# Hybrid trunk layer on one core: the second product of each seven-product unit moved up, branch weights fetched a tile ahead, the last row's norm at high priority

## The chip, the core and the metric

The kernel runs on one core of a Trainium2 chip, in one launch. The metric is the device time of that launch in microseconds (us), as the median of several runs. The kernel before takes 1981.67 us (3 runs, 1977.3 to 1984.02). The engines are called by the names of the profile: PE multiplies matrices (PEld is its loading of weights), DVE, ACT and POOL work on vectors, SP only issues transfers; ACT issues transfers too. An engine works through its own list of instructions in order, and waits between engines are made with semaphores.

## The reference, cut to what matters

One layer of a decoder trunk with 1024 channels, 1024 tokens (16 meta tokens ahead of them) and a feed-forward width of 4096. Four mixers work side by side on the normalised input, each result is projected, weighted with its own gate and summed; an output projection, a residual and a squared-ReLU feed-forward part follow.

```python
h = rmsnorm(x, norm1_g)
proj = jnp.einsum('bld,dc->blc', h, w_in)
(..., gate_logits) = jnp.split(proj, split_at, axis=-1)
branches = (hgrn2_mixer(...), multiscale_pool(...), stick_breaking_attention(...), short_conv_mixer(...))
gates = jax.nn.sigmoid(gate_logits.astype(F32)).reshape(B_, L, N_BRANCH, D_MODEL)
mixed = jnp.zeros((B_, L, D_MODEL), F32)
for n in range(N_BRANCH):
    mixed = mixed + gates[:, :, n] * jnp.einsum('blw,wd->bld', branches[n], w_branch[n]).astype(F32)
x = x + jnp.einsum('bld,de->ble', mixed.astype(x.dtype), w_o)
h2 = rmsnorm(x, norm2_g)
act = jnp.square(jax.nn.relu(jnp.einsum('bld,df->blf', h2, w_up)))
return x + jnp.einsum('blf,fd->bld', act, w_down)
```

The output is the norm of the last x, without the leading tokens.

## The kernel before

Every large matrix is held as a rounded part and a remainder (`hi` and `lo`, made by a cast on ACT, L77, and a subtraction on DVE, L78), so that a product of two blocks is three matmuls: hi by hi, hi by lo, lo by hi. The stages come one after the other: mixers, gates, branches (each mixer's result times its `w_branch`, times its gate, summed in `mixed`), output projection, up projection, down projection.

**The seven-product unit.** In the gates and in the up projection the product of a weight block and the activations is done by a scheme of Strassen's kind, in units of a 256 by 1024 result, `strassen_run`. A unit has seven products of 12 matmuls each (4 blocks along the inner axis, 3 matmuls for each), all matmuls 128x512, in three accumulators of PSUM: `al_` (tag mm, 3 buffers), `be` (tag z, 2 buffers), `ga` (tag tr, 2 buffers). Products 1, 6, 7 and 4 go into `al_`, one upon the other, 5 and 3 into `be`, 2 into `ga`. ACT copies what stands in an accumulator between two products (`keep_copy`, L720): c1 after product 1, c5 after product 5, c2 after product 6. The next product may go into the accumulator only when the copy is made: product 6 waits for c1, product 7 for c2, product 3 for c5. The four quarters of the result are taken out by `put`: (0,0) from `ga` and c1, (1,1) from `al_` and c5, (0,1) from `be` and c2, (1,0) from `al_` alone.

In the code the products stand as 1, 5, 6, 2, 7, 3, 4. There are 20 units in the gates stage and 14 in the up stage. `ahead()` in the middle of a unit writes the load of the next unit's weights (`strassen_load`): two transfers on SP's queue (`raw` a, L685, and `raw` b, L687), then additions and casts that make the seven left operands: `hi` and `lo` for products 1 and 2, `sh` and `sl` for 5 and 6 and, in a second pair, for 3 and 7, `eh` and `el` for 4. POOL does the additions (L692 to L697), and a buffer of `raw` is free for the next load when they are done.

**The list of each engine.** The order in which an engine works through its instructions is fixed when the kernel is built: a scheduler goes through the instructions of all engines by a priority that follows the order of the code, and takes on each engine what its own estimate finds ready first. So a product may stand elsewhere in PE's list than in the code, and two products may be interleaved.

**After a unit.** In the gates stage ACT applies the sigmoid and sends each result of 128x1024 to DRAM (L852). In the up stage ACT applies relu (L990, L993) and the square (L998), DVE makes three sums (L1004 to L1007), and ACT issues seven transfers of 256 KB to `sum_dram` (L1012), the left operands of the down projection's own seven products.

**The branches.** For each of four branches, `load_branch` reads the branch's four blocks of 128x1024 (`raw` or `sf` to `b_hi` and `b_lo`), and for each of eight tiles of 128 channels `load_branch_w` reads a weight tile (`cc`, 3 buffers, to `eh` and `el`, 2 buffers each); 24 matmuls in two chunks, and DVE multiplies with the gate (`go`, read back from `gate_dram`, L877) into `mixed` (L884).

**The end.** The down projection's last unit, `Unit.end`, normalises the last rows in `final`: a square sum on ACT, a few small operations, two multiplications and the transfers of the output.

Of the kernel before, what the change touches and what calls it, by code (L numbers as in the profile page):

```python
# [20 lines left out]
KD = D // P  # L21
# [26 lines left out]
def hybrid_trunk_kernel(ctx: ExitStack, tc: tile.TileContext, x_tok, metas, vecs, gains, w_in, w_br, w_pool,  # L48
# [21 lines left out]
    def new(pl, shape, dt, tag, bufs=None):  # L70
        return pl.tile(shape, dt, tag=tag, name=nm(tag), **({} if bufs is None else {"bufs": bufs}))
# [136 lines left out]
    with ExitStack() as st:  # L208
# [222 lines left out]
        for i in range(NS + 2):  # L431
            parts, z, r = [], iter(()), i % (2 * NB)
# [272 lines left out]
    def strassen_run(pl, lhs, hi, lo, th, tl, put, ahead, tail=None):  # L705
        def blk(k0, c0):
            return hi[:, k0:k0 + 4, c0:c0 + 512], lo[:, k0:k0 + 4, c0:c0 + 512]

        rhs = {1: blk(0, 0), 2: blk(4, 0), 3: blk(4, 512), 4: (th[3], tl[3]), 5: (th[0], tl[0]), 6: (th[1], tl[1]),
               7: (th[2], tl[2])}  # L710

        def prod(ps, i, fresh):
            for k in range(4):
                for n, (x, y) in enumerate(((0, 0), (0, 1), (1, 0))):
                    nc.tensor.matmul(ps, lhs[i][x][:, k, :], rhs[i][y][:, k, :], start=fresh and k == 0 and n == 0,  # L715
                                     stop=k == 3 and n == 2, skip_group_check=not fresh)

        def keep_copy(ps):
            c = new(pl, [P, 512], F32, "cc", 3)
            nc.scalar.copy(c, ps)  # L720
            return c

        al_, be, ga = bank("mm"), bank("z"), bank("tr")
        prod(al_, 1, True)
        c1 = keep_copy(al_)
        prod(be, 5, True)
        c5 = keep_copy(be)
        nxt = ahead()
        prod(al_, 6, False)
        c2 = keep_copy(al_)  # L730
        prod(ga, 2, True)
        put(0, 0, ga, c1)
        prod(al_, 7, False)
        put(1, 1, al_, c5)
        if tail is None:
            prod(be, 3, False)
            put(0, 1, be, c2)
            prod(al_, 4, False)
            put(1, 0, al_, None)
        else:  # L740
            c7 = keep_copy(al_)
            de = bank("av")
            prod(de, 4, True)
            put(1, 0, de, c7)
            tail()
            prod(be, 3, False)
            put(0, 1, be, c2)
        return nxt
# [33 lines left out]
    with ExitStack() as st:  # L782
# [3 lines left out]
        parts = {}  # L786
# [83 lines left out]
        for i, n in enumerate(order):  # L870
            if i:
                load_branch(i)
            bh, bl = parts[i]
            for dt in range(KD):
                wb = load_branch_w(i, dt) if dt else parts[i, 0]
                sg = new(p2, [P, T], F32, "go", 3)
                nc.sync.dma_start(sg, gate_dram[n, dt])  # L877
                for c0, w in QCH:
                    cs = slice(c0, c0 + w)
                    pb = bank("mm")  # L880
                    for k in range(4):
                        mm3(pb, (wb[0][:, k, :], wb[1][:, k, :]), (bh[k][:, cs], bl[k][:, cs]), k == 0, k == 3)
                    if i == 0:
                        nc.vector.tensor_mul(mixed[:, dt, cs], pb, sg[:, cs])  # L884
                    else:
                        nc.vector.tensor_mul(sg[:, cs], pb, sg[:, cs])
                        nc.vector.tensor_add(mixed[:, dt, cs], mixed[:, dt, cs], sg[:, cs])
# [39 lines left out]
    with ExitStack() as st:  # L927
# [151 lines left out]
        class Unit:  # L1079
# [37 lines left out]
            def end(self, prev):  # L1117
# [17 lines left out]
                final(self.m + 4, 1)  # L1135
                self.prod(self.be, 3)
                nc.vector.tensor_add(self.acc(0, 1), self.be, self.acc(0, 1))
                final(self.m, 1)

        NU = (NF - FS) // 2  # L1140
        for spot, ps in held:
# [102 lines left out]
```

## Time and profile before

| | before |
|---|---|
| median of 3 runs | 1981.67 us |
| the profiled execution, its own time | 1980.0 us |
| its span in the profile | 1978.2 us |
| PE busy, share of the span | 1931.9 us, 98% |
| mean granted clock of PE, share of full speed | 0.996 |
| gates stage, 20 units (677.0 to 1056.7 us) | 379.7 us, of which PE busy 377.3 |
| first 18.3 us of the branches (1056.7 to 1075.0) | PE busy 16.0 us |
| up stage, 14 units (1374.7 to 1641.1) | 266.4 us, of which PE busy 266.4 |

The span runs from the first to the last instruction of the profiled execution; its own time is 1.8 us more. A row of the timeline gives the start of an instruction, its duration, engine and line, what it writes and reads, and in brackets how long its engine stood idle ahead of it and what released it. A group of matmuls on PE overlaps: each lasts some 0.39 us and the next starts 0.227 us later when nothing is waited for, so that a product of 12 takes 2.72 us and a unit of 84 takes 19.04 us.

### The profile page before, as it was taken

Reading aid. Unit: us, or ns where it says so; the run is one execution under the profiler, and the core shown is the slowest. Engines: PE = TensorE matmul, PEld = TensorE weight load, DVE = VectorE, ACT = ScalarE, POOL = GpSimd, SP = SyncE. Lnnn points to the kernel's source line nnn. Section 1 sums busy time; section 2 is a strip of 40 time slices with the busy share of each in tenths; the row PEclk is TensorE's granted clock in tenths of the full one; section 3 lists DMA queues with packets and bytes.
Section 4 is the critical chain, followed back from the end, with each engine's and each line's share of the span. In section 5 each row is a group of like instructions: output and inputs, shape, how many; then the busy total and the mean of one; then the engine's idle time right before and its main releaser. Section 6 shows DMA issues by size and latency. Waiting matters only on the chain.

```text
span 1978.2 us, 25779 instructions
## 1 busy us (share of the span) xinstructions
PE 1931.9 (98%) x9974; PEld 1647.4 (83%) x9974; DVE 1291.9 (65%) x1783; ACT 844.0 (43%) x1452; POOL 329.1 (17%) x280
## 2 busy tenths in 40 slices
PE   8999999999999999999999999999999999999998
PEld 7889899988899888888887888888888887777876
DVE  6677877666768844344334667479555546888887
ACT  6556654233324433333342112255544544343445
POOL 1000001111000033333320000000323212322322
PEclk9999999999999999999999999999999999999999
DMA  3000101110102233333326554242454557343433
GB/s 140 33 33 22 43 33 49 54 43 26 40 33 91 85 149 117 139 123 112 128 104 231 186 187 169 77 143 93 136 170 138 155 165 258 127 145 135 152 138 137
DMA packets 112076, 224.61 MB, mean 114 GB/s; under 512 B 8129, under 2 KB 58817, under 8 KB 111954
## 3 DMA queue, kind: packets, MB, share of 16 engines
q1 hardware_dynamic: 56706, 175.22, 25.9%
q10 hardware_dynamic: 55248, 47.75, 7.2%
q8 instruction: 78, 1.28, 0.3%
q14 instruction: 44, 0.36, 0.1%
HBM read 157.40 MB, written 65.54 MB: 113 GB/s over the span
## 4 chain that ended last, share of the span: by engine, by line
PE 76%; DVE 9%; issue 9%; DMA 3%; ACT 2%; POOL 1%; POOLq 0%; DVEq 0%; ACTq 0%; SPq 0%
PE mm L715 18%; PE mm L104 9%; PE mm L103 9%; PE mm L102 9%; PE z L715 9%; PE tr L715 5%; PE mm L1092 3%; PE z L1092 2%; PE av L362 1%; PE z L582 1%; DVE wb L78 1%; PE tr L1092 1%; DVE keep L339 1%; DVE wa L78 1%; DMA raw<-in_w_dn_dram 1%
## 5 line engine op out<-in xcount | busy, mean ns | idle before, releaser
L102 PE MATMUL mm<-h_hi,hi 128*128 128x384 f32 (+4 forms) x880 | 303.0, 345 | 1.4 <-DVE a L198 1.0
L103 PE MATMUL mm<-h_lo,hi 128*128 128x384 f32 (+4 forms) x880 | 295.2, 336 | 1.1 <-DVE h_lo L78 1.1
L104 PE MATMUL mm<-h_hi,lo 128*128 128x384 f32 (+4 forms) x880 | 295.8, 336 | 0.0
L103 PEld LDWEIGHTS mm<-h_lo,hi 128*128 128x128 f32 x880 | 166.6, 189 | 7.9 <-DVE h_lo L78 1.9
L104 PEld LDWEIGHTS mm<-h_hi,lo 128*128 128x128 f32 x880 | 166.0, 189 | 8.0
L102 PEld LDWEIGHTS mm<-h_hi,hi 128*128 128x128 f32 x880 | 166.0, 189 | 7.9 <-DVE a L198 1.4
L78 DVE TENSOR_TENSOR sl<-sf,sh 128x1024 fp32r<-128x1024 f32 x68 | 83.8, 1232 | 128.8 <-ACT sh L77 128.8
L692 POOL TENSOR_TENSOR sf<-raw 128x512 f32<-128x512 f32 x30 | 40.3, 1342 | 764.1 <-DMA raw<-in_w_up_dram 459.3
L78 DVE TENSOR_TENSOR lo<-raw,hi 128x1024 fp32r<-128x1024 f32 x76 | 95.7, 1259 | 45.2 <-ACT hi L77 44.8
L77 ACT CAST hi<-raw 128x1024 fp32r<-128x1024 f32 x76 | 79.9, 1052 | 77.0 <-PE mm L103 40.7
L715 PE MATMUL mm<-th,sh 128*128 128x512 f32 x272 | 106.2, 390 | 0.0
L77 ACT CAST sh<-sf 128x1024 fp32r<-128x1024 f32 x68 | 71.4, 1052 | 81.3 <-PE z L715 41.7
L715 PE MATMUL mm<-tl,sh 128*128 128x512 f32 x272 | 105.8, 389 | 0.0
L715 PE MATMUL mm<-th,sl 128*128 128x512 f32 x272 | 105.8, 389 | 0.0
L339 DVE TENSOR_TENSOR_SCAN keep<-keep 128x1040 f32<-128x1040 f32 (+3 forms) x64 | 88.9, 1390 | 25.7 <-ACT keep L332 18.9
L102 PE MATMUL mm<-b_hi,eh 128*128 128x512 f32 x256 | 99.6, 390 | 1.8 <-DVE mixed L884 1.8
L103 PE MATMUL mm<-b_lo,eh 128*128 128x512 f32 x256 | 100.1, 391 | 0.1
L104 PE MATMUL mm<-b_hi,el 128*128 128x512 f32 x256 | 99.6, 390 | 0.5 <-DVE el L78 0.5
L78 DVE TENSOR_TENSOR el<-raw,eh 128x512 fp32r<-128x512 f32 x34 | 36.2, 1064 | 64.5 <-ACT eh L77 61.3
L334 POOL TENSOR_SCALAR_AFFINE_SELECT keep<-keep 128x128 f32<-128x128 f32 x64 | 22.3, 348 | 300.2 <-ACT keep L332 260.2
L77 ACT CAST at_h<-tr 128x384 fp32r<-128x384 f32 (+2 forms) x112 | 54.5, 495 | 36.6 <-PE tr L349 34.9
L77 ACT CAST s_hi<-s_raw 128x1280 fp32r<-128x1280 f32 x28 | 35.4, 1266 | 80.9 <-DMA s_raw<-sum_dram 45.8
(439 smaller groups left out, 5019.2 us busy)
## 6 DMA issues: line engine op xcount, KB each, us to landing
raw<-in_w_in_dram SPq DMA_DIRECT2D x76, 512.0 KB, 3.7
s_raw<-sum_dram SPq DMA_DIRECT2D x28, 896.0 KB, 4.8
gate_dram<-go ACTq DMA_DIRECT2D x32, 512.0 KB, 2.6
go<-gate_dram SPq DMA_DIRECT2D x32, 512.0 KB, 3.7
raw<-in_w_up_dram SPq DMA_DIRECT2D x32, 512.0 KB, 3.8
raw<-in_w_dn_dram SPq DMA_DIRECT2D x29, 512.0 KB, 4.4
sum_dram<-go ACTq DMA_DIRECT2D x52, 256.0 KB, 4.7
sum_dram<-sums ACTq DMA_DIRECT2D x39, 256.0 KB, 4.8
```

Of the source, the lines that this page charges most:

```text
L77: nc.scalar.copy(hi, src)
L78: (eng or nc.vector).tensor_sub(lo, src, hi.bitcast(F32))
L102: nc.tensor.matmul(ps, lh, rh, start=first, stop=False)
L103: nc.tensor.matmul(ps, lh, rl, start=False, stop=False)
L104: nc.tensor.matmul(ps, ll, rh, start=False, stop=last)
L334: nc.gpsimd.affine_select(out=t[:, :P], in_=t[:, :P], compare_op=ALU.is_gt, fill=1.0, base=0, pattern=[[1, P]], channel_multiplier=-1)
L339: nc.vector.tensor_tensor_scan(t, t, t, 1.0, op0=ALU.mult, op1=ALU.min)
L362: nc.tensor.matmul(av[:, :w], pair.vv[e][:, b, :], a[:, b, :w], start=i == 0 and a is at[0], stop=i == len(order) - 1 and a is at[1])
L582: nc.tensor.matmul(ps[:, c * 64:(c + 1) * 64], xc, low, start=True, stop=True)
L692: eng.tensor_add(s12[:, 0], a21, a22)
L715: nc.tensor.matmul(ps, lhs[i][x][:, k, :], rhs[i][y][:, k, :], start=fresh and k == 0 and n == 0, stop=k == 3 and n == 2, skip_group_check ...
L1092: nc.tensor.matmul(ps, x, y[:, rs], start=fresh and k == 0 and n == 0, stop=k == 1 and n == 2, skip_group_check=not fresh)
```

## The change

It has three parts. In `strassen_run` product 2 and the `put` of (0,0) are written directly behind product 1, so that the order in the code is 1, 2, 5, 6, 7, 3, 4. In the branches the load of a tile's weights is written one tile earlier, ahead of the tile's gate load and matmuls. The last `final` of the kernel stands in a block of high priority, which lets the scheduler take its instructions before others that are ready.

```diff
@@ strassen_run
         al_, be, ga = bank("mm"), bank("z"), bank("tr")
         prod(al_, 1, True)
         c1 = keep_copy(al_)
+        prod(ga, 2, True)
+        put(0, 0, ga, c1)
         prod(be, 5, True)
         c5 = keep_copy(be)
         nxt = ahead()
         prod(al_, 6, False)
         c2 = keep_copy(al_)
-        prod(ga, 2, True)
-        put(0, 0, ga, c1)
         prod(al_, 7, False)
         put(1, 1, al_, c5)
@@ branches
             for dt in range(KD):
-                wb = load_branch_w(i, dt) if dt else parts[i, 0]
+                wb = parts.pop((i, dt))
+                if dt + 1 < KD:
+                    parts[i, dt + 1] = load_branch_w(i, dt + 1)
                 sg = new(p2, [P, T], F32, "go", 3)
@@ Unit.end
-                final(self.m, 1)
+                with tc.high_priority():
+                    final(self.m, 1)
```

Lines of the changed kernel stand two or three further down than those of before from L878 on: L884 becomes L886, L990 L992, L998 L1000, L1012 L1014.

**PE in a gates unit.** PE's list around product 7 of a unit in the middle of the gates stage. The names are accumulator, left operand, right operand: `h_hi_93` is the activations (products 1, 2 and 3), `th` and `tl` their sums (the others), `sh` and `sl` the weights' sums. Before, where product 2 ends and product 7 begins:

```order
L715 MATMUL tr_8692<-h_hi_93,hi_8595 128x512
L715 MATMUL tr_8692<-h_lo_94,hi_8595 128x512
L715 MATMUL tr_8692<-h_hi_93,lo_8596 128x512
L715 MATMUL mm_8690<-th_887_5926,sh_8609 128x512 [waits Activation_49]
L715 MATMUL mm_8690<-tl_890_5929,sh_8609 128x512
L715 MATMUL mm_8690<-th_887_5926,sl_8610 128x512 [waits DVE_49]
```

And of the change, from the end of product 6 to the beginning of product 7 of the same unit:

```order
L715 MATMUL mm_8690<-tl_889_5928,sh_8617 128x512
L715 MATMUL mm_8690<-th_886_5925,sl_8618 128x512
L715 MATMUL z_8691<-h_hi_93,sh_8623 128x512 [waits Activation_49]
L715 MATMUL z_8691<-h_lo_94,sh_8623 128x512
L715 MATMUL z_8691<-h_hi_93,sl_8624 128x512 [waits DVE_49]
L715 MATMUL z_8691<-h_hi_93,sh_8623 128x512
L715 MATMUL z_8691<-h_lo_94,sh_8623 128x512
L715 MATMUL z_8691<-h_hi_93,sl_8624 128x512
L715 MATMUL z_8691<-h_hi_93,sh_8623 128x512
L715 MATMUL mm_8690<-th_887_5926,sh_8623 128x512 [waits Activation_49]
L715 MATMUL mm_8690<-tl_890_5929,sh_8623 128x512
```

All 12 matmuls of product 2 stood between 6 and 7 before; after, seven matmuls of product 3 stand there (its other five come between 7 and 4), in every unit of the gates and of the up stage but the last of either. Only the first unit of the gates is in PE's list as it was: there the list of before has 1, 2, 5, 6, seven of 3, 7, five of 3, 4 as well. In the up stage the first matmuls of the next unit's product 1 (one in the second unit, one more in each that follows) come to stand between products 5 and 6 of a unit.

**ACT in an up unit.** ACT's list from the result quarter (1,0) of one unit to the copies of the next, early in the up stage; `cc<-mm` is c1 or c2, `cc<-z` is c5, the DMA rows are the transfers to `sum_dram`, of which `go_12088`, the last, is the seventh; a DMAHW in brackets is a wait for an earlier transfer with the same semaphore. Before:

```order
L998 ACTIVATE go_12088<-go_12088 128x1024 [waits Activation_49]
L720 COPY cc_12246<-mm_12231 128x512 [waits PE_49]
L1012 DMA sum_dram<-go_12088 128x4x128 [waits Activation_49]
L1012 DMA sum_dram<-go_12087 128x4x128 [waits DMAHW1_49,DVE_49]
L1012 DMA sum_dram<-sums_12217 128x4x128 [waits DMAHW2_49,DVE_49]
L1012 DMA sum_dram<-sums_12217 128x4x128 [waits DVE_49]
L1012 DMA sum_dram<-go_12088 128x4x128 [waits DMAHW4_49]
L720 COPY cc_12260<-z_12232 128x512 [waits PE_49]
L77 CAST eh_12284<-raw_12264 128x512
L77 CAST sh_12274<-sf_12270 128x1024 [waits PE_49,Pool_49]
L720 COPY cc_12300<-mm_12231 128x512 [waits PE_49]
```

Of the change:

```order
L77 CAST eh_12298<-raw_12278 128x512 [waits DMAHW6_49,PE_49]
L992 ACTIVATE go_12088<-mm_12089 128x512 [waits PE_49]
L1014 DMA sum_dram<-go_12087 128x4x128 [waits Activation_49]
L1000 ACTIVATE go_12088<-go_12088 128x1024 [waits Activation_49]
L1014 DMA sum_dram<-sums_12217 128x4x128 [waits DVE_49]
L1014 DMA sum_dram<-go_12088 128x4x128 [waits Activation_49]
L1014 DMA sum_dram<-go_12087 128x4x128 [waits DMAHW2_49,DVE_49]
L1014 DMA sum_dram<-sums_12217 128x4x128 [waits DMAHW3_49,DVE_49]
L1014 DMA sum_dram<-sums_12217 128x4x128 [waits DVE_49]
L1014 DMA sum_dram<-go_12088 128x4x128 [waits DMAHW5_49]
L720 COPY cc_12246<-mm_12231 128x512 [waits PE_49]
L720 COPY cc_12274<-z_12232 128x512 [waits PE_49]
```

The copy c1 (`cc_12246`) stood ahead of the last five transfers, and stands behind all seven. The transfer that the seventh waits for (same semaphore) is another one too: before, `raw` b of the next weights; after, `raw` a, whose cast `hi` follows in ACT's list behind c1. The seventh transfer of each of the first twelve units is like that, and c1 stands behind it in units 2 to 13. Between c5 and c2 ACT now also has the cast `hi` and a relu; the relu of (1,1) stands ahead of the second `sh` cast, where before it was the cast of `hi` that stood ahead of both.

**DVE at the start of the branches.** DVE's list in the first tiles of the first branch; `mixed` rows multiply with the gate, `el` is the remainder of a weight tile, `b_lo` that of a branch block, those with 977x and 978x belonging to the second branch. Before:

```order
L884 TENSOR_TENSOR mixed_9487<-mm_9490,go_9488 128x512 [waits DMAHW7_49,PE_49]
L884 TENSOR_TENSOR mixed_9487<-mm_9504,go_9488 128x512 [waits PE_49]
L78 TENSOR_TENSOR el_9521<-cc_9518,eh_9520 128x512 [waits DMAHW1_49,DVE_49,Activation_49]
L78 TENSOR_TENSOR el_9557<-cc_9554,eh_9556 128x512 [waits DMAHW3_49,DVE_49,Activation_49]
L78 TENSOR_TENSOR b_lo_9773<-sf_9770,b_hi_9772 128x1024 [waits DMAHW0_49,Activation_49]
L78 TENSOR_TENSOR b_lo_9785<-sf_9782,b_hi_9784 128x1024 [waits DMAHW1_49,Activation_49]
L884 TENSOR_TENSOR mixed_9487<-mm_9526,go_9524 128x512 [waits DMAHW2_49,PE_49]
```

Of the change:

```order
L78 TENSOR_TENSOR el_9491<-cc_9488,eh_9490 128x512 [waits DMAHW1_49,DVE_49,Activation_49]
L886 TENSOR_TENSOR mixed_9487<-mm_9496,go_9494 128x512 [waits DMAHW7_49,PE_49]
L886 TENSOR_TENSOR mixed_9487<-mm_9510,go_9494 128x512 [waits PE_49]
L78 TENSOR_TENSOR el_9527<-cc_9524,eh_9526 128x512 [waits DMAHW5_49,DVE_49,Activation_49]
L78 TENSOR_TENSOR b_lo_9773<-sf_9770,b_hi_9772 128x1024 [waits DMAHW6_49,Activation_49]
L886 TENSOR_TENSOR mixed_9487<-mm_9532,go_9530 128x512 [waits DMAHW1_49,PE_49]
```

The second tile's `el` stood behind the first tile's two multiplications and stands ahead of them; of the second branch's two `b_lo` ahead of the second tile's multiplications only one is left. On SP's queue the second branch's second block is now read after three more gate tiles. Ahead of these rows, at the very start, the first tile's `el` has moved behind one `b_lo`.

At the end of the kernel no engine's list differs between the two kernels: the block of high priority moves nothing.

## Rows read from the trace of the kernel before

**Rows 1.** The page, part 1: busy us (share of span), instructions.

```profile
PE 1931.9 (98%) x9974; PEld 1647.4 (83%) x9974; DVE 1291.9 (65%) x1783; ACT 844.0 (43%) x1452; POOL 329.1 (17%) x280
```

**Rows 2.** Windows: gates and up stage; busy us per engine, clock, DMA share, GB/s.

```profile
677.00:1056.70 379.70, 377.31 (x1658) 311.71 (x1657) 161.47 (x163) 149.80 (x214) 112.18 (x72) 1.00 0.34 125
...
1374.70:1641.10 266.40, 266.40 (x1177) 220.63 (x1177) 141.34 (x160) 134.79 (x185) 68.26 (x48) 1.00 0.52 151
```

**Rows 3.** Timeline of PE, first gates unit; then the window behind it, columns as above.

```profile
679.80 0.80 PE L715 MATMUL z<-th,sh 128*128 128x512 f32 x1 [2.39 <-ACT sh L77]
...
679.80:683.30 3.50, 3.50 (x9) 2.68 (x10) 3.43 (x4) 3.47 (x4) 0.00 (x0) 0.57 0.59 222
```

**Rows 4.** Timeline, first unit of the gates, seven of product 3, then product 7.

```profile
686.79 0.39 PE L715 MATMUL z<-h_hi,sh 128*128 128x512 f32 x1
...
686.81 1.05 ACT L77 CAST sh<-sf 128x1024 fp32r<-128x1024 f32 x1 [1.72 <-PE mm L715]
...
687.76 0.57 ACT L720 COPY cc<-mm 128x512 f32<-128x512 f32 x1
...
688.15 0.39 PE L715 MATMUL z<-h_hi,sh 128*128 128x512 f32 x1
688.39 0.19 PEld L715 LDWEIGHTS mm<-th,sh 128*128 128x128 f32 x1 [0.28 <-ACT cc L720]
...
688.73 0.39 PE L715 MATMUL mm<-tl,sh 128*128 128x512 f32 x1
```

**Rows 5.** Timeline of ACT, end of one up unit and start of the next.

```profile
1448.21 1.05 ACT L77 CAST sh<-sf 128x1024 fp32r<-128x1024 f32 x1 [1.19 <-PE z L715]
...
1453.85 0.57 ACT L720 COPY cc<-mm 128x512 f32<-128x512 f32 x1
1453.97 1.09 ACTq L1012 DMA_DIRECT2D sum_dram<-go  x2
1455.43 1.54 ACTq L1012 DMA_DIRECT2D sum_dram<-sums  x2
1457.01 1.32 ACTq L1012 DMA_DIRECT2D sum_dram<-go  x1
1458.37 0.59 ACT L720 COPY cc<-z 128x512 f32<-128x512 f32 x1 [3.95 <-issue]
```

**Rows 6.** Timeline of PE, same stretch: first matmul of products 1 and 6.

```profile
1450.90 0.39 PE L715 MATMUL mm<-h_hi,hi 128*128 128x512 f32 x1
...
1456.34 0.39 PE L715 MATMUL mm<-th,sh 128*128 128x512 f32 x1
```

**Rows 7.** Timeline of POOL, then of SP's queue, same stretch.

```profile
1451.85 1.74 POOL L697 TENSOR_TENSOR sf<-raw,sf 128x512 f32<-128x512 f32 x1
...
1453.62 0.33 SPq L685 DMA_DIRECT2D raw<-in_w_up_dram  x1
1460.23 0.33 SPq L687 DMA_DIRECT2D raw<-in_w_up_dram  x1
```

**Rows 8.** L685 in the up stage (12 transfers): issue to landing.

```profile
DMA to landing us min/median/max: 3.5/4.3/5.8
```

**Rows 9.** Transfers in the up stage by line: KB each, median us to landing.

```profile
sum_dram<-sums ACTq DMA_DIRECT2D x39, 256.0 KB, 4.8
```

**Rows 10.** Waits of PE, 1056.7 to 1075 us: us in total, times, longest.

```profile
PE mm L102 <- DVE mixed L884: 1.8, 1, 1.8
PE mm L104 <- DVE el L78: 0.5, 1, 0.5
```

**Rows 11.** Timeline of DVE, start of the branches.

```profile
1062.29 1.37 DVE L884 TENSOR_TENSOR mixed<-mm,go 128x512 f32<-128x512 f32 x2 [1.10 <-PE mm L104]
1063.58 1.28 DVE L78 TENSOR_TENSOR el<-cc,eh 128x512 fp32r<-128x512 f32 x2
1070.46 2.51 DVE L78 TENSOR_TENSOR b_lo<-sf,b_hi 128x1024 fp32r<-128x1024 f32 x2 [5.59 <-ACT b_hi L77]
```

**Rows 12.** Timeline of SP's queue, start of the branches.

```profile
1064.41 5.00 SPq L877 DMA_DIRECT2D go<-gate_dram  x3
```

## The prediction

> **What bounds the kernel now.** I read the page first: PE is busy for 98% of the span, DVE, at 65%, is next [rows 1]. A sum over the whole kernel doesn't say what a stage loses, so I went to the windows of the two stages with seven-product units. In the up stage PE's busy time equals the window: 266.4 of 266.4 us; in the gates 377.3 of 379.7 [rows 2]. All of the gates' idle time is one wait at the first unit's product 5, 2.39 us for the cast `sh`; in the 3.5 us behind it the granted clock is 0.57 (mostly the lower level, 1.2 of 2.4 GHz) and 9 matmuls run, 1.46 us more than 9 x 0.227 [rows 3]. So the reader is to see that units 2 to 20 of the gates and all of the up stage lose nothing now. An order of products can't gain there; it can only lose. What can be gained lies at the first unit and at the start of the branches, where PE waits 1.8 us for `mixed` and 0.5 us for `el` [rows 10].
>
> **Product 2 in the gates.** No matmul is added, removed or resized. The first unit stays as it is in PE's list, so its wait of 2.39 us stays: gain 0. For the other units the trace of before has a sample, because the first unit ran in the new order. Between products 6 and 7 product 2 gave ACT 12 matmuls, 2.72 us, for the copy c2; now seven of product 3 give 7 x 0.227 = 1.59 us. When product 6 ends, at 686.79, ACT begins the next `sh` cast (its buffer is read by 6), 1.05 us, and only then copies c2, 0.57 us, from 687.76. The weight load of product 7 waits 0.28 us for it, to 688.39, and the matmul behind starts 0.34 us after the first, not 0.227 [rows 4]. From the last matmul of product 3 (688.15) to the second of 7 (688.73) there are 0.58 us where 2 x 0.227 = 0.45 would do: 0.13 us lost, with the next row's rounding 0.15. The order on ACT is the same in each unit (`sh`, then c2), so I take 0.15 x 18 units = +2.7 us. Its lower end is 0, if c2 just makes it; its upper end 0.3 for a unit, +5.4, if the semaphores fall less luckily.
>
> **Product 2 in the up stage.** The same short cover costs 0.15 x 12 = +1.8 us (0 to 3.6).
>
> The larger matter is c1. Let T be the end of product 4, 1450.90 in the shown unit [rows 6]. Before, ACT copied c1 at 1453.85 for 0.57 us, to T + 3.5, and product 6 began at 1456.34, T + 5.44: 1.9 us to spare [rows 5, 6]. In the new list c1 stands behind all seven transfers to `sum_dram`. Product 6 is now due after products 1, 2 and 5 and one matmul of the unit after, 37 x 0.227 = 8.4 us after T, or 36 where one is fewer: I use 8.28. Before, the last issue began at 1457.01 and lasted 1.32 us, to T + 7.43 [rows 5]. With c1 behind it, 7.43 + 0.05 + 0.57 = T + 8.05: 0.2 us to spare, if that were all.
>
> It isn't, because the seventh transfer now waits for the landing of `raw` a. Before, that load was issued at 1453.62, T + 2.72, as POOL ended its second addition [rows 7]. That chain begins with the second `sh` cast at 1448.21, T - 2.69 [rows 5]; the relu of (1,1), about 0.6 us, now stands ahead of it. Product 7 now ends five matmuls before product 3 does, T - 2.72 - 1.13 = T - 3.85; an addition on DVE and the relu follow, for pieces as large as the copy c1, 0.57 us [rows 5], so with hand-overs some 0.7 each (my estimate), and the cast begins at some T - 2.3. POOL and the load are 0.4 us later: T + 3.15. The load lands 4.3 us after issue, 3.5 to 5.8 [rows 8]. It travels among the sums, which take 4.8 [rows 9], and `raw` b, which went out 6.6 us behind it (1460.23) [rows 7], now goes right behind. I take the sums' figure, nearer to a crowd: T + 7.9. Then an issue (0.4 to 1.3, say 0.45) and c1: 7.9 + 0.45 + 0.57 + 0.05 = T + 8.97. That is 0.7 us late; the restart adds 0.11 as in [rows 4]: 0.8 us for each of units 2 to 13, 12 x 0.8 = +9.6 us. Ends: with a landing after 3.5 us c1 comes at T + 7.7, cost 0; with 5.8 us it is late by 1.6, with the restart 1.7, +20 us.
>
> The row of the long issue also meets a rule. Five issues from 1453.97 on took 1.09 + 1.54 + 1.32 = 3.95 us of ACT's time, and the c5 copy behind them waited as long [rows 5]. The Trainium skill's page "DMA: Bandwidth & Descriptors", section "Issuing engines are not separate DMA queues", says that initiating a transfer takes the sequencer a time that "is usually small relative to the DMA itself". By that, seven issues ahead of c1 would cost next to nothing and this term would be 0, the sum +3.8; here the trace disagrees, with 3.95 us of issuing beside 4.8 us of landing. I go by the trace.
>
> **The ends of the stages.** In the last up unit c2 stands behind a cast that waits for a row's load; from the 4.3 us of [rows 8] against cover of a product or two I estimate +1.0 (0 to 3). In the first units of both stages another order of casts gives 0 to 0.6: +0.3.
>
> **Branch weights.** `el` of the second tile stood behind two multiplications (from 1062.29), and ran at 1063.58 [rows 11]; now it stands ahead of them, its data there as `cc` is loaded early: the wait of 0.5 us and its restart go, -0.6. The wait of 1.8 us came from DVE's list: two `b_lo` of the second branch, released by ACT at 1070.46 after 5.59 us of idling and running until 1072.97, stood ahead of the second tile's `mixed`, whose accumulator PE needed [rows 11]. Now one `b_lo` stands there, so some 1.2 us go at least, and both perhaps; but the gate tile must be in too, and its load's issue, 1064.41, waits for its write as before [rows 12]. Against this the first tile's `el` comes behind one `b_lo`, up to 1.2 us later. I take -1.4 for the pair: together -2.0 us, from -2.8 (all of [rows 10] with two restarts) to +0.5 (the first tile's delay and nothing gained).
>
> **The last norm.** No engine's list differs there, so nothing is hidden or shortened: 0.
>
> **Sum.** +2.7 + 1.8 + 9.6 + 1.0 + 0.3 - 2.0 = +13.4 us. The profiled execution took 1980.0 us, so 1993.4; that one is 1.7 below the median of 1981.67, to which I add the same: **1995 us**.
>
> **Rivals.**
> *c1 is in time.* The lateness is the difference of two figures near 8 us: with a landing at the fast end, or sums sent less densely, it vanishes, and what is left is 13.4 - 9.6 = +3.8, some 1985.5 us. For it: the 3.5 us of the minimum, and the 0.2 us to spare without the wait. Against it: the median of 4.3 still gives 3.15 + 4.3 + 0.45 + 0.62 = T + 8.5, late by 0.25 and a restart, +4 us over the 12 units. Chance 0.22.
>
> *c1 is later still.* Each late copy pushes the transfers of its unit together with both loads. Landing at 5.8 us, or an issue of 1.3 us in place of 0.45, makes 1.7 us a unit: 12 x 1.7 = 20, in place of 9.6: 2005 us. Waits as long as that of [rows 3], 2.39 us, would bring the lower clock as well, 1.46 us each time; three such would make 2009, and six 2014. Chance 0.15.
>
> *Faster.* The moved product pays only if the first unit's wait goes. If the casts of that unit came earlier with the changed lists, 2.39 + 1.46 us, in all about 4 us, would be saved, with -2.8 at the branches, and no unit lost anything at products 6 and 7: 1975 us. It decides if c2 is copied within 1.59 us of product 6's end and c1 before T + 8.3. Against it: [rows 4] show c2 late in the same order, and the first unit's list is unchanged. Chance 0.07.
>
> *The change does nothing* holds for the block of high priority, with near certainty, and is in the sum; for the whole it would need all terms at their lower ends, and lies within the first rival.
>
> **How the numbers follow.** The forecast, c1 late by 0.25 to 1.3 us, has 0.56 and covers 1987 to 2001. From no change 0.3%, some 6 us, can be told. Faster by more: 0.07, the third rival. Within it (1975.7 to 1987.6): the first rival, 0.22, and a little of the forecast's lower edge, 0.02: 0.24. Slower: 0.69. The range reaches from 1982 to 2008: out of it are the third rival (0.07), the first rival's lower part (0.04) and the tail of the second (0.06).
>
> **What would show it.** In the changed kernel's up stage the waits of PE should list "mm L715 <- ACT cc L720" some 24 times, half with 0.5 to 1 us at product 6 and half with 0.2 to 0.3 at product 7; the timeline of ACT should have c1 right behind an issue, 8.5 us or more after product 4's end, and a seventh issue that begins at the landing of L685's load. The up window should grow by 12 us, the gates' by 3. At the branches both rows of [rows 10] should be gone or shorter. I'm wrong if c1 begins before T + 7.7 in most units, if the first unit of the gates no longer waits, or if PE waits for something else in the middle of the gates, where the cast `hi` now stands ahead of c5 and is covered only as long as its load lands early.

## The result, and the profile after

| | before | after |
|---|---|---|
| median | 1981.08 us (4 runs) | 1995.72 us (4 runs, 1994.97 to 1999.94) |
| ratio to before, 95% interval | | 1.0075 [1.0062, 1.0089] |
| span of the profiled execution | 1978.2 us | 1993.4 us, 15.2 longer |
| PE busy, share of the span | 98% | 97% |
| mean granted clock | 0.996 | 0.997 |

The change makes the kernel slower by 0.75%. The windows of the changed kernel, cut at the same matmuls as those of [rows 2], with the stretches between them added, say where (columns as there):

```profile
677.13:1059.49 382.36, 379.69 (x1658) 309.16 (x1656) 160.02 (x162) 146.67 (x213) 97.69 (x72) 1.00 0.34 124
1059.49:1376.83 317.34, 314.91 (x1410) 258.08 (x1409) 216.35 (x322) 101.61 (x153) 0.00 (x0) 1.00 0.46 160
1376.83:1653.79 276.96, 272.88 (x1177) 218.69 (x1177) 151.35 (x160) 132.26 (x185) 67.83 (x48) 1.00 0.51 144
1653.79:1993.40 339.61, 317.70 (x1370) 256.32 (x1368) 279.47 (x378) 142.60 (x210) 95.30 (x64) 0.99 0.45 155
```

Beside before's, of which the two that [rows 2] lack stand here:

```profile
1056.70:1374.70 318.00, 315.08 (x1410) 258.08 (x1409) 216.45 (x322) 102.25 (x153) 0.00 (x0) 1.00 0.46 160
...
1641.10:1978.20 337.10, 317.36 (x1370) 256.45 (x1368) 279.36 (x377) 142.23 (x210) 94.68 (x64) 0.99 0.45 155
```

So the gates grew by 2.7 us, the up stage by 10.6, everything between them shrank by 0.7, and the down stage, whose instructions are the same, grew by 2.5. In the up stage PE's busy time is no longer that of the window, and PE's waits name one cause. This is the list of waits of PE in the up window, then that of its weight loads, which carry the wait for a free accumulator (us in total, times, longest):

```profile
PE mm L715 <- ACT cc L720: 3.7, 11, 0.5
```

```profile
PEld mm L715 <- ACT cc L720: 12.5, 24, 0.9
PEld z L715 <- ACT cc L720: 0.6, 1, 0.6
```

24 waits for a copy, twelve at product 6 and twelve at product 7. One of the former, in ACT's timeline of one unit:

```profile
1461.69 1.35 ACTq L1014 DMA_DIRECT2D sum_dram<-sums  x2
1464.80 0.37 ACTq L1014 DMA_DIRECT2D sum_dram<-go  x1
1465.21 0.58 ACT L720 COPY cc<-mm 128x512 f32<-128x512 f32 x1 [6.03 <-DMA raw<-in_w_up_dram]
1465.69 0.59 ACT L720 COPY cc<-z 128x512 f32<-128x512 f32 x1
1466.17 1.06 ACT L77 CAST hi<-raw 128x1024 fp32r<-128x1024 f32 x1
```

The sixth issue ends at 1463.05, the seventh begins only at 1464.80, and c1 stands behind it with 6.03 us of idling put down to the landing of `raw`. That load's row on SP's queue, the time to landing of the eleven such loads in units 2 to 12 (the first unit's took 3.5 us), and the matmuls of PE that waited:

```profile
1459.82 0.33 SPq L685 DMA_DIRECT2D raw<-in_w_up_dram  x1
```

```profile
DMA to landing us min/median/max: 4.7/4.8/5.0
```

```profile
1465.00 0.39 PE L715 MATMUL mm<-h_hi,hi 128*128 128x512 f32 x1
1465.85 0.50 PE L715 MATMUL mm<-th,sh 128*128 128x512 f32 x1 [0.46 <-ACT cc L720]
1466.19 0.40 PE L715 MATMUL mm<-tl,sh 128*128 128x512 f32 x1
```

1459.82 + 4.8 = 1464.6, then the hand-over and the seventh issue. In unit 13 no such load is left, and the seventh issue stands behind a load of the down stage. Product 6 begins 0.85 us after the matmul ahead of it, where 0.227 would do: 0.62 us lost, and 0.11 more at the next.

### The profile page after: what moved, and what is told of

The parts are those of the page before. It is cut to its first block, busy times and chain, and to the rows that moved or that the text cites. A ratio compares the mean times of both kernels' runs of the same rounds, so it can differ in the third digit from the quotient of the medians.

```text
span 1993.4 us, 25820 instructions
## 1 busy us (share of the span) xinstructions
PE 1940.8 (97%) x9974; PEld 1642.8 (82%) x9974; DVE 1300.6 (65%) x1783; ACT 837.9 (42%) x1452; POOL 314.9 (16%) x280
## 4 chain that ended last, share of the span: by engine, by line
PE 67%; DVE 12%; issue 8%; DMA 6%; ACT 4%; POOL 2%; SPq 0%; ACTq 0%; DVEq 0%; POOLq 0%
PE mm L715 15%; PE mm L104 9%; PE mm L103 9%; PE mm L102 9%; PE z L715 7%; PE mm L1094 3%; PE tr L715 3%; DMA raw<-in_w_up_dram 2%; PE av L362 2%; PE z L1094 2%; PE z L582 1%; DMA s_raw<-sum_dram 1%; DVE wb L78 1%; PE tr L1094 1%; DVE wa L78 1%
## 5 line engine op out<-in xcount | busy, mean ns | idle before, releaser
L715 PE MATMUL mm<-th,sh 128*128 128x512 f32 x272 | 111.1, 408 | 3.9 <-ACT cc L720 3.7
L720 ACT COPY cc<-mm 128x512 f32<-128x512 f32 x70 | 40.7, 582 | 112.9 <-DMA raw<-in_w_up_dram 53.2
L715 PEld LDWEIGHTS mm<-th,sh 128*128 128x128 f32 x272 | 51.0, 187 | 27.8 <-ACT cc L720 18.2
```

## The experiments

Each kernel was timed in five rounds beside the kernel before; ratios are to before, with their 95% interval. Stage times are windows of the profiled execution, cut at the same matmuls.

**c1 ahead of the transfers.** The changed kernel, with

```diff
-        def keep_copy(ps):
+        def keep_copy(ps, first=False):
             c = new(pl, [P, 512], F32, "cc", 3)
-            nc.scalar.copy(c, ps)
+            if first:
+                with tc.high_priority():
+                    nc.scalar.copy(c, ps)
+            else:
+                nc.scalar.copy(c, ps)
             return c
...
-        c1 = keep_copy(al_)
+        c1 = keep_copy(al_, True)
```

> The changed kernel with one difference: the copy c1 of each unit is written at high priority, so ACT's list has it ahead of the last six transfers to sum_dram in place of behind all seven; the first matmuls of the next unit are no longer interleaved, and c2 still stands behind the sh cast. My theory (product 6 is late by 0.6 us in twelve up units because c1 stands behind a transfer that waits for the landing of raw a): product 6's loss goes, product 7's 0.15 us stays, so the up stage is 2 to 3.5 us longer than before in place of 10.6, and the time is some 7 us under that of the change: 1988 to 1989.5 us. Rival (the new order of products itself, or the transfers' load on memory, costs the 10 us): no difference, 1994 to 1998.

Measured: 1.0154 [1.0140, 1.0168], 2013.9 us: 18 us slower than the change by the medians, 16 by the ratios, against both expectations. Product 6 loses nothing any more, as the theory has it, but the up stage takes 291.4 us, 25.0 over before. Its weight loads' waits there:

```profile
PEld z L715 <- ACT cc L724: 15.7, 12, 2.4
PEld mm L715 <- ACT cc L724: 10.6, 13, 0.9
```

The wait has moved to product 3 (z), and to product 7 behind it. ACT's timeline shows c5, the last row, behind the same seventh transfer and a relu:

```profile
1464.73 0.59 ACT L722 COPY cc<-mm 128x512 f32<-128x512 f32 x1 [0.58 <-PE mm L715]
1464.73 1.57 ACTq L1018 DMA_DIRECT2D sum_dram<-go  x2
1466.67 2.33 ACTq L1018 DMA_DIRECT2D sum_dram<-sums  x3
1469.03 2.51 ACTq L1018 DMA_DIRECT2D sum_dram<-go  x1
1472.41 0.63 ACT L999 ACTIVATE go<-go 128x512 f32<-128x512 f32 x1 [7.10 <-DVE go L998]
1472.95 0.57 ACT L724 COPY cc<-z 128x512 f32<-128x512 f32 x1
```

In the changed kernel c5 stood right behind c1, ahead of cast and relu; with c1 gone ahead, the scheduler put the relu between the issues and c5. So c1's place was a cause, but freeing it alone uncovers the next copy in the same list. Two things end late ahead of c5 here, the seventh issue (1471.54) and the relu, whose addition on DVE waits for earlier transfers out of its buffer.

**Six issues on ACT.** The changed kernel, with the third transfer of each up unit but the last issued by POOL:

```diff
-                eng.dma_start(dst[:, i], t.rearrange("p (m t) -> p m t", m=4))
+                (nc.gpsimd if i == 2 and f + 2 < NF else eng).dma_start(dst[:, i], t.rearrange("p (m t) -> p m t", m=4))
```

> The changed kernel with one of the seven transfers of each up unit but the last issued by POOL in place of ACT. c1 still stands behind all transfers that ACT issues (six), but the last of them shares no semaphore with raw a any more and doesn't wait for its landing. My theory (the wait for the landing makes c1 late): product 6's loss goes entirely, since the sixth issue then ends some 6 us after the unit's start: up stage 2 to 3.5 us longer than before, time 1988 to 1989.5 us. Rival (standing behind so many issues makes c1 late, the landing only coincides): one issue of 0.37 us fewer leaves some 0.2 of 0.6 us in each of twelve units and the restart, up stage 6 to 7 us longer than before, 1991.5 to 1993.

Measured: 1.0043 [1.0029, 1.0056], 1991.6 us; up stage 272.8 us, 6.4 over before. ACT's timeline in one unit:

```profile
1461.28 1.40 ACTq L1014 DMA_DIRECT2D sum_dram<-sums  x2
1462.72 0.59 ACT L720 COPY cc<-mm 128x512 f32<-128x512 f32 x1 [3.96 <-PE tr L715]
1464.44 1.05 ACT L77 CAST hi<-raw 128x1024 fp32r<-128x1024 f32 x1 [1.13 <-DMA raw<-in_w_up_dram]
1466.30 0.63 ACT L995 ACTIVATE go<-go 128x512 f32<-128x512 f32 x1 [0.81 <-DVE go L994]
1466.84 0.57 ACT L720 COPY cc<-z 128x512 f32<-128x512 f32 x1
```

c1 follows the sixth issue at once, and no product 6 of the stage is late: with one issue fewer and no shared semaphore the whole 0.63 us of a unit goes, not the 0.4 that one issue takes. That is the theory's side on product 6. The edit takes away an issue and the shared semaphore together; the sizes tell them apart. The stage time agrees with the rival's 6 to 7, but from another place: the wait for the landing now stands at the cast `hi`, 1.13 us, ahead of c5, and product 3 loses 5.5 us over the stage, up to 1.2 in one unit. The landing of `raw` a matters wherever in ACT's list something waits for it.

**All issues on SP.** The changed kernel, with `eng = nc.sync` for all seven transfers of every unit.

> The changed kernel with all seven transfers of every up unit issued by SP in place of ACT, so that no copy stands behind an issue; c1 is early, and in ACT's list a relu of quarter (0,0) stands ahead of c5, its addition waiting for earlier transfers out of the same buffer to land. The kernel with c1 first lost 25 us in the up stage, at product 3 and then product 7. Theory now (the wait for the buffers, brought forward with quarter (0,0), makes c5 late): product 3 still loses, up stage 5 to 15 us over before, 1989 to 2000 us. Rival (the issues on ACT ahead of c5 cost it): up stage 2 to 3.5 us over before, only product 7's share, 1987 to 1989.

Measured: 1.0024 [1.0013, 1.0035], 1986.6 us. The up window:

```profile
1377.62:1646.49 268.87, 268.87 (x1177) 219.47 (x1176) 152.52 (x160) 133.87 (x184) 67.80 (x48) 1.00 0.50 150
```

2.5 us over before, all of it in front of product 7: the rival's figure. No product 6 and no product 3 is late. Of the 10.6 us of the change 8.1 are therefore the price of issuing these transfers, with their waits, from the engine that also makes the copies. The expectation, that a relu's wait for buffers would still cost product 3, falls: it is there (0.58 us in front of the relu), but c5 comes in time. SP also sends the sums earlier, so how much of the first experiment's wait at c5 was the issue and how much the buffers stays open.

**c2 made by DVE.** The changed kernel, with `nc.vector.tensor_copy` for c2.

> The changed kernel with the copy c2 made by DVE in place of ACT, so that it stands behind no sh cast; as a consequence the scheduler also puts c1 ahead of five of the seven transfers and all of product 3 or four of its matmuls ahead of product 7. My theory (product 7 loses 0.15 us in 31 units because c2 stands behind a cast that begins when product 6 ends): both losses of the units go, gates stage as long as before (379.7 us, the wait of 2.4 us at its first unit included), up stage within 1 us of before, time 1980 to 1983 us. Rival (the short cover costs product 7 its 0.15 us whoever copies, since DVE's own list holds c2 up as well): gates 2 to 4 us longer than before, time 1984 to 1988.

Measured: 1.0109 [1.0095, 1.0123], 2004.6 us; gates 382.7 us, as in the change, up stage 287.0. A miss: the copy then stands in DVE's list behind a remainder that waits for ACT's cast, and product 7 waits for it, as DVE's timeline and PE's row show:

```profile
1471.45 1.23 DVE L78 TENSOR_TENSOR lo<-raw,hi 128x1024 fp32r<-128x1024 f32 x1 [1.52 <-ACT hi L77]
1472.59 0.68 DVE L720 COPY cc<-mm 128x512 f32<-128x512 f32 x1
```

```profile
1473.33 0.50 PE L715 MATMUL mm<-th,sh 128*128 128x512 f32 x1 [1.40 <-DVE cc L720]
```

It doesn't settle what product 7 waited for in the change; the next two do.

**The gates alone.** The kernel before, with product 2 moved up only in the units of the gates (a flag of `strassen_run`).

> The kernel before with product 2 moved up in the 20 units of the gates alone; up stage, branches and end as before. My theory: product 7 loses 0.15 us in 18 units since c2 stands behind a cast, gates stage 2.6 to 2.9 us longer, up stage 266.4 us as before: 1984 to 1986 us, some 0.13% over before. Rival (the stages aren't separate: what the up stage lost in the changed kernel begins with the state that the gates leave): up stage longer by 3 us or more, 1988 and above.

Measured: 1.0020 [1.0011, 1.0029], 1985.5 us; the windows of gates and up stage:

```profile
677.31:1059.69 382.38, 379.70 (x1658) 309.14 (x1656) 159.85 (x162) 146.82 (x213) 97.78 (x72) 1.00 0.34 124
...
1376.40:1642.80 266.40, 266.40 (x1177) 220.63 (x1177) 141.65 (x160) 135.01 (x185) 68.65 (x48) 1.00 0.52 151
```

The gates take what they take in the change, the up stage what it took before. The stages are separate.

**The gates alone, c2 ahead of the cast.** As the last, with

```diff
-                for n, (x, y) in enumerate(((0, 0), (0, 1), (1, 0))):
+                for n, (x, y) in enumerate(((1, 0), (0, 0), (0, 1)) if i == 6 else ((0, 0), (0, 1), (1, 0))):
...
-        c2 = keep_copy(al_)
+        c2 = keep_copy(al_, True)
```

with `keep_copy` as in the kernel with c1 ahead.

> As the kernel before with product 2 moved up in the gates alone, and c2 put ahead of the sh cast in ACT's list: in product 6 the three matmuls of each block run with the remainder first, so that the weights' rounded part is read last and the cast can't start ahead of c2, and c2 has high priority. The scheduler then leaves four matmuls of product 3, 0.91 us, between products 6 and 7 in place of seven. My theory (the cast ahead of c2 costs product 7 its 0.15 us): c2 needs 0.57 us and two hand-overs, some 0.85 in all, so product 7 is in time or late by 0.1 at most: gates stage 379 to 381 us, 0 to 1 us over before. Rival (the cover between 6 and 7 is simply too short for a copy, whatever stands ahead): four matmuls in place of seven cost 0.7 us more a unit, gates stage 12 us and more over before.

Measured: 1.0010 [1.0000, 1.0019], 1984.0 us. Product 7 has only four matmuls of cover in place of seven, and its weight load waits less. PE around one product 7, from the last of the four to the second of product 7:

```profile
879.63 0.39 PE L715 MATMUL z<-h_hi,sh 128*128 128x512 f32 x1
879.85 0.43 PE L715 MATMUL mm<-th,sh 128*128 128x512 f32 x1
880.12 0.40 PE L715 MATMUL mm<-tl,sh 128*128 128x512 f32 x1
```

From 879.63 to 880.12 there are 0.49 us, 0.04 over two spacings; in [rows 4] 0.13. Over units 2 to 20 the spacings above 0.22667 us add up to 1.25 us, against 3.47 in the kernel without this edit. So most of the loss is the cast ahead of c2, not the length of the cover, and the rival's 12 us are excluded. The gates stage as a whole took 381.9 us in this execution, above the 379 to 381 expected: its first 83 matmuls took 24.0 us against 22.3 in the kernel without the edit, with a granted clock of 0.51 from 682.1 to 685.6 us. The medians, 1985.5 and 1984.0, have overlapping intervals; it is the spacings that decide.

**Branch weights alone.** The kernel before with part two of the change.

> The kernel before with the branch weights a tile ahead and nothing else. As the changed kernel's trace has it: the waits at the start of the branches lose 2.7 us in place of 3.2, a gain of 0.5 us: 1980 to 1982 us, not to be told from before. My forecast's term was -2.0: 1978.5 to 1980. Rival (the later growth of the changed kernel's down stage, 2.4 us, comes from the branches' other order of transfers): 1982.5 to 1984.

Measured: 1.0004 [0.9995, 1.0013]: no difference. The stretch from the branches to the up stage took 317.5 us, between the 318.0 and 316.9 of the lists of before in the two profiles shown here.

**The last norm alone.** The kernel before with part three.

> The kernel before with the last norm at high priority and nothing else. Every engine's list is that of before, so the time should be that of before within 0.15%, and what its profile shows in the down projection beside that of before is the spread between executions of the same program: the changed kernel's down stage was 2.4 us longer than before, and if that is spread this one should differ by 1 us or more somewhere in it too. Rival (those 2.4 us come from the high priority): 1984 to 1985.

Measured: 1.0002 [0.9993, 1.0011]: no difference, as lists without a difference demand. Its profile is that of before's instructions a second time, and shows what two executions differ by:

```profile
679.00:1057.85 378.85, 376.17 (x1658) 310.61 (x1657) 160.24 (x163) 149.71 (x214) 112.94 (x72) 1.00 0.35 125
1057.85:1374.73 316.88, 314.89 (x1410) 258.09 (x1409) 216.21 (x322) 102.26 (x153) 0.00 (x0) 1.00 0.47 160
1374.73:1641.12 266.39, 266.39 (x1177) 220.62 (x1177) 141.50 (x160) 134.86 (x185) 68.51 (x48) 1.00 0.52 150
1641.12:1980.43 339.31, 317.43 (x1370) 256.32 (x1368) 280.32 (x377) 142.02 (x210) 95.85 (x64) 0.99 0.45 155
```

Against before's: the gates begin 2.0 us later, and take 0.85 less (all in the first unit), branches 1.1 less, up stage the same to 0.01, down stage 2.2 more.

**Both causes taken out.** The changed kernel with the issues on SP and c2 ahead of the cast in both stages.

> The changed kernel with both causes taken out: the seven transfers of an up unit issued by SP, and in both stages product 6 with the remainder first and c2 at high priority, so that c2 stands ahead of the sh cast. If these two are all that the moved product cost, the gates behind their first unit take some 357.3 us (as with c2 first in the gates alone; 356.1 before, 359.6 in the change) and the up stage 266.3 to 267.5 (268.8 with SP's issues alone, 276.9 in the change): 1982 to 1985 us, within 0.2% of before. If the c2 order costs something else in the up stage, where ACT has more to do, up is 269 or more and the time above 1986.

Measured: 1.0025 [1.0012, 1.0038], 1986.5 us. By the windows: gates 381.0 us, 2.1 over the 378.9 of the same lists as before; up stage 267.8, 1.4 over. Of the 14 us that the change lost in these two stages some 3.5 are left, about 0.1 at each product 7. The median lies 1.5 us above what was expected; the interval's lower end, 1.0012, is 1984.7 us.

**The kernel before, a little better.** Before with part two, and the short convolution's first step on ACT (`nc.scalar.mul` in place of a product on DVE).

> The kernel before with the branch weights a tile ahead, and the first step of the short convolution (a product with a vector, 0.75 us on DVE) done by ACT, so that DVE reaches the first gates unit's additions sooner; product order as before. The first unit waited 2.39 us and then ran 3.5 us at a granted clock of 0.57. With 0.7 us less to wait the lower clock should not come: first unit 28.0 to 28.7 us in place of 29.5 to 30.4, total 1.5 to 3 us under before, 1979 to 1980.5. If the wait ends elsewhere (the cast's other inputs), no change.

Measured: 1.0007 [0.9997, 1.0017]: no gain. The first unit's wait stays at 2.2 us, so DVE's 0.75 us were not what it was waiting for. The granted clock behind it was 1.00, as the expectation had it, but it was 1.00 behind waits of 2.38 and 2.39 us too, in the change and in the last norm alone. ACT's timeline suggests another cause:

```profile
678.04 0.58 ACT L720 COPY cc<-mm 128x512 f32<-128x512 f32 x1 [3.76 <-DMA br_dram<-b]
678.52 2.00 ACT L77 CAST sh<-sf 128x1024 fp32r<-128x1024 f32 x2
```

The first unit's c1 writes a `cc` tile in memory that an outgoing transfer of the stage before still reads. By the profile it waits for that to land, and both casts of `sh` wait behind it in ACT's list. The next experiment tests this.

**Another layout of the gates' pool.** The kernel before, with the tiles of that pool in another order of memory (`sh`, `sl`, `sf`, `cc`, `go`, `eh`, `el`; before `go`, `cc`, `sf`, `sh`, `sl`, `eh`, `el`), so that c1 and the first `sh` need wait for no landing:

```diff
-        reserve(p2, *STRASSEN_TAGS)
+        reserve(p2, *[STRASSEN_TAGS[j] for j in (3, 4, 2, 1, 0, 5, 6)])
```

> The kernel before, with the tiles of the gates' pool laid out in another order of memory (sh and sl first, then sf, cc, go), and nothing else. In the kernel before, the first copy of the first gates unit (c1, at 678.21) waits 3.52 us for the landing of the transfer br_dram<-b, whose memory cc takes over, and the casts of sh stand behind it in ACT's list. Theory: c1 and the first sh then wait for no landing, so PE's wait of 2.39 us in the first unit falls to 0.3 to 1.5 us (sl still waits for one transfer to land, and with it product 3 and those behind), 1979.5 to 1981 us, a ratio of 0.9992 to 0.9998. Rival: sl, or the remainder's landing, stands where c1 stood, and the wait goes to a later product of the same unit: first unit as long as before, ratio 1.000.

Measured: 0.9986 [0.9977, 0.9996], 1979.6 us. ACT's timeline there, and PE's waits from 676 to 710 us:

```profile
674.89 0.59 ACT L720 COPY cc<-mm 128x512 f32<-128x512 f32 x1
677.28 1.05 ACT L77 CAST sh<-sf 128x1024 fp32r<-128x1024 f32 x1 [1.80 <-DVE sf L693]
```

```profile
PE z L715 <- ACT sh L77: 0.8, 1, 0.8
PE mm L715 <- ACT cc L720: 0.6, 1, 0.6
PE z L715 <- DVE sl L78: 0.3, 1, 0.3
```

c1 ends without a wait, and the cast now waits for DVE's sums, so the landing is shown to be the cause. The 2.7 us of the last norm alone, whose lists are before's (2.4 for `sh`, 0.3 for `sl`), become 1.7 in three places. The same 83 matmuls from the first unit on take 21.5 us, against 22.3 there and 23.1 in the profile of before, which has the lower clock: the waits account for 0.8, and the rest of the 1.6 is the clock. The median fell by 2.9 us. What of it lies beyond the first unit is no more than two executions differ by in the down stage, and isn't traced.

**The layout and the branch weights.** The same with part two of the change.

> The same layout with part two of the change (branch weights a tile ahead), the two edits that cost nothing alone. Theory: the two add up, the first gates unit shorter by 1 to 2 us and the branches by 0 to 1: 1978.5 to 1981 us, ratio 0.9985 to 0.9998. Rival: no gain from either, ratio 1.000 within its interval, and the kernel before stays the best.

Measured: 0.9987 [0.9978, 0.9996], 1980.0 us: no more than by the layout alone, so part two adds nothing that can be told. The layout is the one edit here that beats the kernel before, by 0.04 to 0.23%, and it has nothing to do with the order of the products.

## Why the prediction was right, step by step

The forecast was 1995 us, from a sum of +13.4; measured were 1995.7, and 15.2 in the profiled execution. The terms:

| term | forecast | measured | from |
|---|---|---|---|
| product 7 in the gates | +2.7 | +3.5 | gates window less the 378.85 of the same lists as before |
| product 7 in the up stage | +1.8 | +2.6 | spacings of product 7 and of the restart behind it |
| c1 in the up stage | +9.6 | +7.6 | spacings of product 6, 0.42 to 0.80 a unit in twelve units |
| last up unit, first units | +1.3 | +0.4 | product 3 of the second up unit; the last unit 0 |
| branch weights | -2.0 | -0.7, not to be told from 0 | window; the same lists differ by 1.1 |
| last norm | 0 | 0 | tail after the last matmul unchanged |
| down stage | none | +2.5 | same instructions; 336.7 to 342.1 us over the kernels here |

**Bound.** Right: nothing could be gained in the units, since nothing was lost there, and the first unit kept its list and its wait of 2.4 us. The lower clock of [rows 3] did not follow that wait in the changed kernel. PE's row there, and the window behind it:

```profile
679.93 0.50 PE L715 MATMUL z<-th,sh 128*128 128x512 f32 x1 [2.38 <-ACT sh L77]
```

```profile
679.93:683.43 3.50, 3.21 (x13) 2.36 (x14) 3.02 (x4) 3.47 (x4) 0.00 (x0) 1.00 0.63 250
```

The granted clock is 1.00 here, where [rows 3] has 0.57 behind the same wait. So a wait of this length doesn't always bring the lower level, as the second rival took for granted. What it costs the unit is not the 1.46 us of nine matmuls either: at the full clock PE waits 0.29 us for `sl`, with a restart behind it, and the whole unit is 0.85 us shorter. That is why the gates window grew by 2.7 us and the units behind the first by 3.5.

**Product 7.** Right in mechanism: c2 behind the cast that begins when product 6 ends. The sample of [rows 4] held in units 2 to 20 of the gates, 19 in place of the 18 counted; 0.15 became 0.19 on average, as the matmuls behind a restart run a few hundredths late for longer than the two that were counted. The experiment with c2 first shows the cause for all but 1.25 us of it.

**c1.** Right place, right releaser, right size to a quarter. In the shown unit the times against T, the end of product 4 (1456.84, from 1458.88 less the nine matmuls of product 1 that were left): load issued T + 2.98 (forecast 3.15), seventh issue T + 7.96 (7.9), c1 done T + 8.95 (8.97). Product 6 was due at T + 8.39, not at 8.28, which is 0.1 us less to lose; in most other units the landing came a little sooner. The choice of 4.8 us for the landing over the 4.3 of [rows 8] was the step that decided it, and the load landed in 4.7 to 5.0. The kernel with six issues shows that the landing is what c1 waited for. Without that wait c1 would have had more to spare than the 0.2 us of the prediction: the sixth issue ended at T + 6.2, so an issue of 0.37 us and the copy behind it would have been done by some T + 7.2 (an estimate from these rows; seven issues on ACT without the wait were not run). What the prediction didn't see is how near c5 stood to the same fate: put c1 in front and the loss more than doubles.

**A page's rule.** The page "DMA: Bandwidth & Descriptors" of the Trainium skill, section "Issuing engines are not separate DMA queues", calls the time to initiate a transfer usually small beside the transfer itself. The prediction said that the trace disagrees, by the 3.95 us of five issues in [rows 5]. That was a misreading: it sets five issues beside one landing, and each row with x2 also holds the gap between its two issues. Two rows of a view of L1012 in the up stage of before, the single issues of `go` (duration in ns: minimum, median, maximum) and the time to landing of all transfers of the line:

```profile
L1012 ACTq DMA_DIRECT2D sum_dram<-go x52: 366/367/1497, 1393.7 to 1627.5; - x52
...
DMA to landing us min/median/max: 2.3/4.7/6.1
```

So 0.37 us in the median, 1.5 at most, stands beside 4.7 us, and the trace agrees with the page. c1 was late not for the time to initiate, but for the 1.75 us between the end of the sixth issue and the start of the seventh; a rule on the former couldn't set the term to 0. The 8.1 us that SP's issues gave back are no evidence against the page either: they are what issues that wait cost in front of copies that PE needs.

**Branch weights.** The step that failed is "the wait of 1.8 us came from DVE's list, so some 1.2 us go at least". One `b_lo` of the second branch did go from in front of the second tile's `mixed`, but the other stands between the two of the third, waits there for its own late transfer, and PE waits 1.3 us ten microseconds on. DVE's timeline, and PE's row:

```profile
1082.05 1.23 DVE L78 TENSOR_TENSOR b_lo<-sf,b_hi 128x1024 fp32r<-128x1024 f32 x1 [6.65 <-ACT b_hi L77]
1083.19 0.68 DVE L886 TENSOR_TENSOR mixed<-mm,go 128x512 f32<-128x512 f32 x1
```

```profile
1084.02 0.47 PE L102 MATMUL mm<-b_hi,eh 128*128 128x512 f32 x1 [1.28 <-DVE mixed L886]
```

I had looked at the order for the second tile alone.

**Rivals.** c1 in time: excluded by the twelve units whose product 6 was late. c1 later still: no landing over 5.0 us in units 2 to 12, and no lower clock in the up stage. (By its own terms a landing of 5.8 us makes c1 late by 1.74 us, not 1.6, which is 22 us in place of 20.) Faster: the first unit's wait stayed, since it hung on a landing that the change didn't touch. A part of the agreement is luck: the terms' errors (+1.6 on product 7, -2.0 on c1, -0.9 at the ends, +1.3 at the branches) cancel, so that the terms measured give 13.4 again; with the down stage's +2.5 and the first gates unit's -0.85, which the prediction didn't have and which the executions of before's own lists differ by as well, that is the 15.1 by which the two profiled executions differ (1995.1 and 1980.0). The forecast of the profiled execution was 1.7 us too low; that the median was hit more closely, 1995 for 1995.7, is because the 1.7 added for the median turned out as 0.6.

## What to carry to other kernels

A stage whose bounding engine has no idle time can't be improved by another order of its products, but its slack can be spent: look for the copies that sit just in front of their deadline and count what stands ahead of them in their engine's list, transfers' issues too. Where a transfer shares a semaphore with an earlier one, its issue can wait for that one's landing, and everything behind it in the engine's list waits as well. Moving one late item forward can uncover the next in the same list, as it did with c1 and c5; taking the issues off that engine helped both at once, though not c2, which stood behind a cast. At a border between pools, look where the first tiles lie: a copy into memory that a transfer still reads waits for its landing.

## What the runs showed that I had not expected

The up stage, with no wait in it, repeats to 0.01 us (266.39 and 266.40) between executions, and so did units 2 to 20 of the gates, while the down stage took 336.7 to 342.1 us in the kernels here, and the branches differ by about 1 us. The first gates unit differs by the clock: behind a wait of the same 2.4 us the granted clock was 0.57 in one profile of before's lists and 1.00 in the other, and the unit took 23.1 and 22.3 us. So a single profile decides a term in the former stages to hundredths, and can't decide one under 2 us in the latter, in the down stage not one under 5.
